# A feed-forward in two phases: seven block products per pair of weight tiles, and a pass through DRAM between up and down projection

## The chip, the core and the metric

The kernel runs on one core of one Trainium2 chip. The metric is the device time of one execution in microseconds (us), as a median over runs. TensorE (PE) multiplies a stationary 128x128 weight tile with up to 512 moving columns and adds into one of eight PSUM banks. VectorE (DVE), ScalarE (ACT) and GpSimd (POOL) work elementwise on 128 partitions, and SyncE (SP) and ACT issue the DMAs here.

## The reference, cut to what matters

A trunk of two layers works on 1024 latent tokens and 256 context tokens with 1024 features. Each layer has four parallel mixers, an output projection, a second norm and a feed-forward with 2816 hidden features. In the last layer only latent tokens go through the output projection and the feed-forward.

```python
def conv_ffn(h, w_up, conv_w, w_down):
    u, g = jnp.split(h @ w_up, 2, axis=-1)
    return (jax.nn.silu(dwconv(g, conv_w)) * u) @ w_down
...
        x = x + ml[2][:, None] * y_lat
        h2 = modulate(rmsnorm(x, norm2[l]), ml[3][:, None], ml[4][:, None])
        x = x + ml[5][:, None] * conv_ffn(h2, ffn_w_up[l], ffn_conv_w[l], ffn_w_down[l])
```

`dwconv` is a convolution of width 3 along the tokens, for each feature by itself.

## The kernel before, in words

All activations are feature-major: 128 features on the partitions, tokens along the free axis, eight such tiles (KT = 8) for 1024 features. The tokens come in groups (0, 256) context, (256, 512) and (768, 512) latent; the last layer drops the first. The kernel is written in a framework that orders the instructions of each engine ahead of the run, by priority (the order of the program text) and by its own timing model, and gives tiles of one tag a fixed number of buffers. A tile that finds no free buffer waits for the last reader of an old one.

**Products in three passes.** Each float32 operand is split into a float32r part and the rest (`split`: ACT casts `hi`, then POOL or DVE subtracts `lo`). `dense_acc` (L238) adds, for each of the eight feature tiles, hi·hi (L242), hi·lo (L243) and lo·hi (L244). So 24 matmuls make one 128-feature output tile of one token group. `load_w` (L226) loads a weight tile of 128x1024 (512 KB), and splits it: cast at L202, `lo` at L203 on `K.lo_eng`.

**Feed-forward.** `ffn` (L1650) walks over the 22 hidden tiles of 128 in blocks of two. For hidden tile j: the product `g` into `ps_g`, copied by ACT to `gp` (L1671); the convolution `conv3` (one ACT tap at L659, two DVE taps at L662 and L663); a SiLU (L1677); the product `u` into `ps_u`; DVE multiplies it with the convolved gate (L1683) and the result is split into `fh` and `fl`, three buffers each. After two hidden tiles, `down` multiplies both with their rows of `w_down` for all eight output tiles and all groups, and `resid` (L1601) adds each PSUM result, scaled, into the residual `x` in SBUF. The hidden features never leave SBUF. With the last block `done` runs the next norm (or the final norm and the store).

**Around it.** Before the feed-forward of a layer, the output projection (`dense_late`) is done for the first groups, then for the last group, and `norm_mod` normalises a group when its residual is complete. In layer 0, the parameters of the next layer's state-space mixer (`s5.scal`, `mats`, `turns`, `outs`: small DVE operations above all) are computed beside the first nine blocks of the feed-forward: `scal` in one go, the others in steps.

## Time and profile before

| | |
|---|---|
| time, median of 3 runs | 3555.32 us (3553.36 to 3558.95) |
| span of the profiled execution | 3550.2 us |
| feed-forward of layer 0 | about 988 to 1908 us of the span |
| feed-forward of layer 1 | about 2797 to 3527 us of the span |
| PE busy | 3418.2 us (96%) |
| DVE, ACT, POOL busy | 1708.2, 1106.9, 889.9 us |

The profile gives no time of its own for the profiled execution beside its span. The median of the runs is 5.1 us above that span; where a span is turned into a time, these 5.1 us are added. A busy share is an average over stages, so the stages are read one by one.

### The profile page before, as it was taken

Reading aid. Unit: us, or ns where it says so; the run is one execution under the profiler, and the core shown is the slowest. Engines: PE = TensorE matmul, PEld = TensorE weight load, DVE = VectorE, ACT = ScalarE, POOL = GpSimd, SP = SyncE. Lnnn points to the kernel's source line nnn. Section 1 sums busy time; section 2 is a strip of 40 time slices with the busy share of each in tenths; the row PEclk is TensorE's granted clock in tenths of the full one; section 3 lists DMA queues with packets and bytes.
Section 4 is the critical chain, followed back from the end, with each engine's and each line's share of the span. In section 5 each row is a group of like instructions: output and inputs, shape, how many; then the busy total and the mean of one; then the engine's idle time right before and its main releaser. Section 6 shows DMA issues by size and latency. Waiting matters only on the chain. (4 is left out here: it accounts for less than half of the span.)

```text
span 3550.2 us, 48986 instructions
## 1 busy us (share of the span) xinstructions
PE 3418.2 (96%) x19154; PEld 2795.2 (79%) x19186; DVE 1708.2 (48%) x3597; ACT 1106.9 (31%) x1885; POOL 889.9 (25%) x1061
## 2 busy tenths in 40 slices
PE   8899998999999999999999999998999999999998
PEld 6888995676768888888887889985666688888885
DVE  6857727554365486333323563636633432232333
ACT  4224534334242211111223324533333312212222
POOL 1922424011033222222221011331110223323321
PEclk9899998999999999999999999998999999999999
DMA  5577533345111121111112655542153111111111
GB/s 200 166 205 229 156 119 113 110 140 212 65 46 62 54 90 72 36 36 36 42 40 81 162 166 164 142 150 67 60 204 107 42 42 54 53 42 54 48 46 62
DMA packets 264904, 352.84 MB, mean 99 GB/s; under 512 B 89240, under 2 KB 190304, under 8 KB 264672
## 3 DMA queue, kind: packets, MB, share of 16 engines
q1 hardware_dynamic: 168148, 265.90, 23.5%
q10 hardware_dynamic: 96524, 83.81, 7.5%
q8 instruction: 151, 2.47, 0.3%
q14 instruction: 81, 0.66, 0.1%
HBM read 266.09 MB, written 83.52 MB: 98 GB/s over the span
## 5 line engine op out<-in xcount | busy, mean ns | idle before, releaser
L1601 DVE SCALAR_TENSOR_TENSOR x<-pd,modv,x 128x512 f32<-128x512 f32 (+1 forms) x448 | 299.8, 687 | 233.6 <-PE pd L244 233.2
L242 PE MATMUL pd<-fh,wh_d 128*128 128x512 f32 (+1 forms) x896 | 325.3, 369 | 9.3 <-ACT fh L202 5.7
L242 PE MATMUL ps_g<-hb,wh_g 128*128 128x512 f32 (+1 forms) x880 | 326.0, 370 | 3.2 <-ACT hb L214 2.2
L244 PE MATMUL ps_g<-hb,wl_g 128*128 128x512 f32 (+1 forms) x880 | 324.4, 369 | 2.5 <-POOL wl_g L203 2.5
L243 PE MATMUL pd<-fl,wh_d 128*128 128x512 f32 (+1 forms) x896 | 326.0, 367 | 0.7 <-POOL fl L203 0.7
L244 PE MATMUL pd<-fh,wl_d 128*128 128x512 f32 (+1 forms) x896 | 325.5, 368 | 0.0
L242 PE MATMUL ps_u<-hb,wh_u 128*128 128x512 f32 (+1 forms) x880 | 325.4, 370 | 0.0
L243 PE MATMUL ps_g<-hb,wh_g 128*128 128x512 f32 (+1 forms) x880 | 325.1, 369 | 0.0
L243 PE MATMUL ps_u<-hb,wh_u 128*128 128x512 f32 (+1 forms) x880 | 324.7, 369 | 0.0
L244 PE MATMUL ps_u<-hb,wl_u 128*128 128x512 f32 (+1 forms) x880 | 324.3, 369 | 0.2 <-POOL wl_u L203 0.2
L662 DVE SCALAR_TENSOR_TENSOR cv<-gp,vec,cv 128x1281 f32<-128x1281 f32 (+1 forms) x44 | 72.6, 1651 | 476.8 <-ACT cv L659 476.8
L242 PE MATMUL ps_in<-ha,wh_in 128*128 128x384 f32 (+3 forms) x688 | 218.3, 326 | 13.5 <-ACT st L1426 13.5
L203 POOL TENSOR_TENSOR wl_u<-wr_u,wh_u 128x1024 fp32r<-128x1024 f32 x44 | 105.5, 2397 | 481.7 <-ACT wh_u L202 481.7
L243 PE MATMUL ps_in<-ha,wh_in 128*128 128x384 f32 (+3 forms) x688 | 222.4, 323 | 0.0
L244 PE MATMUL ps_in<-ha,wl_in 128*128 128x384 f32 (+3 forms) x688 | 221.2, 322 | 0.0
L242 PE MATMUL ps_in<-hb,wh_in 128*128 128x256 f32 (+1 forms) x704 | 212.7, 305 | 0.8 <-ACT hb L214 0.6
L244 PE MATMUL ps_in<-hb,wl_in 128*128 128x256 f32 (+1 forms) x704 | 212.8, 303 | 0.0
L243 PE MATMUL ps_in<-hb,wh_in 128*128 128x256 f32 (+1 forms) x704 | 212.5, 302 | 0.2 <-DVE hb L215 0.2
L242 PEld LDWEIGHTS pd<-fh,wh_d 128*128 128x128 f32 x896 | 169.1, 189 | 45.8 <-DVE x L1601 7.4
L202 ACT CAST wh_u<-wr_u 128x1024 fp32r<-128x1024 f32 x44 | 46.3, 1051 | 502.4 <-PE pd L243 436.5
L242 PEld LDWEIGHTS ps_g<-hb,wh_g 128*128 128x128 f32 x880 | 166.2, 189 | 36.4 <-ACT hb L214 3.5
L243 PEld LDWEIGHTS pd<-fl,wh_d 128*128 128x128 f32 x896 | 169.4, 189 | 31.9 <-issue 1.7
(509 smaller groups left out, 7691.2 us busy)
## 6 DMA issues: line engine op xcount, KB each, us to landing
wm<-in_w_mod SPq DMA_DIRECT2D x96, 512.0 KB
wr_in<-in_w_in SPq DMA_DIRECT2D x44, 512.0 KB
wr_g<-in_w_up SPq DMA_DIRECT2D x44, 512.0 KB
wr_u<-in_w_up SPq DMA_DIRECT2D x44, 512.0 KB
wr_d<-in_w_down SPq DMA_DIRECT2D x44, 512.0 KB
wr_out<-in_w_out SPq DMA_DIRECT2D x32, 512.0 KB
PF<-st ACTq DMA_DIRECT2D x100, 128.0 KB
PF<-st ACTq DMA_DIRECT2D x60, 192.0 KB
```

The source lines that it names most:

```text
L202: nc.scalar.copy(hi, src)
L203: (eng or nc.gpsimd).tensor_tensor(lo, src, hi.bitcast(F32), OP.subtract)
L242: nc.tensor.matmul(ps, whi(k), ahi(k), start=start and i == 0, stop=False)
L243: nc.tensor.matmul(ps, whi(k), alo(k), start=False, stop=False)
L244: nc.tensor.matmul(ps, wlo(k), ahi(k), start=False, stop=stop and i == len(ks) - 1)
L662: nc.vector.scalar_tensor_tensor(dst, src[:, 0:n], w0, dst, OP.mult, OP.add)
L1601: nc.vector.scalar_tensor_tensor(v, ps, K.modv[l][:, 8 * part + m, c:c + 1], v, OP.mult, OP.add)
```

## The change

The feed-forward becomes two functions. `ffn_up` makes all 22 hidden tiles of a layer and writes each (`u` times gate, float32) to the DRAM tensor `HD`. `ffn_down` reads them back, splits them, and multiplies them with `w_down` in blocks of 1, 3, 4, 4, 4, 4 and 2 hidden tiles. In between, the activations are given up and the residual, which went to the DRAM tensor `XS` after its norm, is loaded again.

In `ffn_up`, hidden tile 0 is made as before. For the other 21, the latent part of the pair (u, g) is a 2x2 block product: rows are the u and the g tile, the inner index is split into features 0-511 and 512-1023 (four tiles each), columns are the two latent groups. Eight block products of twelve matmuls become seven (a Strassen-Winograd scheme). Its weight sums are formed for each tile (four POOL operations on 128x512, then two more splits), its activation sums (`tops`) once in a layer by `norm_fast`, which takes the place of `norm_mod` for the last latent group and works on it in two halves of 256 tokens. Products share two accumulators: `x` receives four of them one after the other without a restart and is copied or added out in between, `z` receives two. The context tokens of layer 0 are multiplied as before, in full.

```diff
-    def dense_acc(self, ps, whi, wlo, ahi, alo, ks, start=True, stop=True):
+    def dense_acc(self, ps, whi, wlo, ahi, alo, ks, start=True, stop=True, check=True):
+    def norm_fast(self, l, xs, kept, act, tops, dsh, pool, t0, n):
...
+        for k in range(4):
+            sh = self.modv[l][:, 28 + k, 0:1]
+            b12, b22 = scaled(k), scaled(4 + k)
+            t1, t4 = kept[k][:, d], kept[4 + k][:, d]
+            t2 = temp(f"n2{k}")
+            nc.vector.tensor_tensor(t1, b12, t1, OP.subtract)
+            stt(t2, b22, sh, t1, OP.add, OP.subtract)
+            self.split(t2, *[v[k][:, d] for v in tops[2]], nc.gpsimd)
+            self.split(t1, hi[k][:, s], lo[k][:, s], nc.gpsimd)
+            stt(b12, b22, dsh[:, k:k + 1], b12, OP.add, OP.subtract)
+            self.split(b12, *[v[k][:, d] for v in tops[3]], nc.gpsimd)
+            h = hi[4 + k][:, s]
+            nc.scalar.activation(h, b22, AF.Identity, bias=sh)
+            stt(lo[4 + k][:, s], b22, sh, h.bitcast(F32), OP.add, OP.subtract)
+            stt(t4, t4, sh, t2, OP.add, OP.subtract)
+            self.split(t4, *[v[k][:, d] for v in tops[4]], nc.vector)
...
-        K.wb = (1, 3)
-        wp = cw.enter_context(pool_(tc, name=f"w3{l}", bufs=3))
+        K.wb = (2, 4)
+        wp = cw.enter_context(pool_(tc, name=f"w3{l}", bufs=4))
...
+            for m in range(4):
+                K.dense(A["w_out"][l, m], act, KT, LAT[1:], resid(x, 2, m), wp, f"out{l}_{m}_768")
+            ws = [K.load_w(A["w_out"][l, m], KT, wp, f"out{l}_{m}_768") for m in range(4, 8)]
+            for t0, n in ((768, 256), (1024, 256)):
+                for m, (hi, lo) in zip(range(4, 8), ws):
...
+                norm(t0, n)
+        K.lo_eng = nc.gpsimd
+        with pool_(tc, name=f"w4{l}", bufs=3) as wq, pool_(tc, name=f"u{l}", bufs=1) as pool:
+            ffn_up(K, l, act, tops, HD, (wp, wq), pool)
+        ct.close()
+        cact.close()
...
+            x = open_x(c3, groups, "xx", side="right")
+            for t0, n in groups:
+                nc.sync.dma_start(x[t0], XS[:, :, t0:t0 + n])
+            s5s = s5[1] if l == 0 else None
+            stages = [(None, 0), (s5s.scal, 0), (s5s.mats, 8), (lambda p: s5s.turns(p, eng=nc.vector), 8), (s5s.outs, 8)] if s5s else []
+            with pool_(tc, name=f"f{l}", bufs=1) as pool:
+                for i, (b0, b1) in enumerate(((0, 1), (1, 4), (4, 8), (8, 12), (12, 16), (16, 20))):
...
+            if not last:
+                cact, act = open_act(f"c{l}")
+            with pool_(tc, name=f"fz{l}", bufs=1) as pool, pool_(tc, name=f"ez{l}", bufs=1, side="right") as ep:
+                ffn_down(K, l, range(NFF - 2, NFF), groups, lambda m: resid(x, 5, m), HD, wp, pool, iter(()), done(x, act), ep)
-def ffn(K, l, act, groups, resid, done, s5, wp):
...
+def ffn_up(K, l, act, tops, HD, wps, pool):
...
+        ur, gr = load("u", j), load("g", NFF + j)
+        uw = split("u", ur)
+        if j:
+            s12 = raw("s")
+            gt(s12[:, 4:], gr[:, :4], gr[:, 4:], OP.add)
+            gt(s12[:, :4], s12[:, 4:], ur[:, :4], OP.subtract)
+            w12 = split("s12", s12, 0, nc.vector)
+            gt(ur[:, :4], ur[:, :4], gr[:, :4], OP.subtract)
+            gt(ur[:, 4:], ur[:, 4:], s12[:, :4], OP.subtract)
+            w34 = split("s34", ur, 0, nc.vector)
+        gw = split("g", gr, 0 if full or not j else 4)
...
+            x = bank(K.pd, "px")
+            prod(x, uw, 0, B11, True)
+            put(ua, x)
+            y = bank(K.pb, "py")
+            prod(y, uw, 4, B21, True)
+            add(ua, y)
+            if full:
+                context(bank(K.pa, "pcu")[:, :TC], uw, u[:, :TC])
+            prod(x, w12, 0, tops[2], False)
+            put(ub, x)
+            z = bank(K.pb, "pz")
+            prod(z, w12, 4, T1, True)
+            put(gb, z)
+            prod(x, w34, 0, tops[3], False)
+            add(gb, x)
+            prod(z, w34, 4, B22, False)
+            add(ub, z)
+            prod(x, gw, 4, tops[4], False)
+            put(ga, x)
+            if full:
+                context(bank(K.pa, "pcg")[:, :TC], gw, gp[:, 1:1 + TC])
...
+        nc.scalar.dma_start(HD[j][:, h0:], u[:, h0:])
+def ffn_down(K, l, js, groups, resid, HD, wp, pool, steps, done=None, spool=None):
...
+    for j in js:
+        raw = pool.tile([P, T], F32, tag="hr", name=f"hr{l}_{j}", bufs=2)
+        nc.sync.dma_start(raw[:, h0:], HD[j][:, h0:])
+        wd.append(K.load_w(A["w_down"][l, j], KT, pool if j % 3 == 0 and not done else wp, f"d{l}_{j}"))
+        h = pool.tile([P, T], F32R, tag="fh", name=f"fh{l}_{j}", bufs=2 if done else 6)
+        lo = pool.tile([P, T], F32R, tag="fl", name=f"fl{l}_{j}", bufs=2 if done else 6)
+        for t0, n in groups:
+            s = slice(t0, t0 + n)
+            K.split(raw[:, s], h[:, s], lo[:, s], nc.vector)
...
+        for m in range(KT):
+            for t0, n in groups:
+                down(m, t0, n)
+            next(steps, None)
```

In `ffn_up`, `prod` is twelve matmuls (four feature tiles, three passes), `put` an ACT copy out of PSUM, `add` a DVE addition out of PSUM into the same place. The rest of the diff takes comments out, cuts the buffers of the loaded mixer outputs (`yraw`) from four to two, and makes the scratch space for DMA descriptors smaller.

## Rows read from the trace of the kernel before

**Rows 1.** The page, busy time and share of each engine.

```profile
PE 3418.2 (96%) x19154; PEld 2795.2 (79%) x19186; DVE 1708.2 (48%) x3597; ACT 1106.9 (31%) x1885; POOL 889.9 (25%) x1061
```

**Rows 2.** Windows: span; busy PE, PEld, DVE, ACT, POOL; clock; DMA.

```profile
988.00:1908.00 920.00, 908.09 (x4741) 774.07 (x4740) 432.58 (x958) 212.73 (x281) 245.95 (x221) 0.99 0.15 51
...
2680.00:2797.00 117.00, 112.94 (x457) 79.79 (x455) 45.99 (x50) 39.92 (x55) 13.49 (x11) 0.98 0.27 95
2797.00:3527.00 730.00, 726.03 (x3198) 592.46 (x3196) 244.07 (x288) 177.32 (x217) 213.59 (x171) 0.99 0.13 45
```

**Rows 3.** Timeline of PE in layer 0: start, duration (us), line, operation.

```profile
1042.27 0.28 PE L243 MATMUL ps_u<-hb,wh_u 128*128 128x256 f32 x1
...
1044.42 0.28 PE L243 MATMUL ps_u<-hb,wh_u 128*128 128x256 f32 x1
...
1045.12 0.39 PE L243 MATMUL ps_u<-hb,wh_u 128*128 128x512 f32 x1
...
1054.88 0.39 PE L244 MATMUL ps_u<-hb,wl_u 128*128 128x512 f32 x1
```

**Rows 4.** Waits of PE, 990 to 1100 and 1300 to 1400: total, times, longest.

```profile
PE pd L242 <- ACT fh L202: 5.7, 1, 5.7
...
PE pd L242 <- DVE x L1601: 3.6, 1, 3.6
```

**Rows 5.** Waits of PE 2660 to 2830, then one window (columns of rows 2).

```profile
PE ps_g L242 <- ACT hb L214: 2.2, 1, 2.2
...
2800.00:2810.00 10.00, 10.00 (x34) 7.79 (x34) 9.12 (x14) 4.27 (x7) 0.00 (x0) 0.72 0.00 0
```

**Rows 6.** Groups by form: count, busy us, mean ns, idle before.

```profile
L1601 DVE SCALAR_TENSOR_TENSOR x<-pd,modv,x 128x512 f32<-128x512 f32 x344 | 253.6, 749 | 211.5 <-PE pd L244 211.3
...
L203 DVE TENSOR_TENSOR wl_in<-wr_in,wh_in 128x1024 fp32r<-128x1024 f32 x44 | 56.2, 1277 | 51.2 <-ACT wh_in L202 50.5 <-PE ps_in L244 0.5
...
L1601 DVE SCALAR_TENSOR_TENSOR x<-pd,modv,x 128x256 f32<-128x256 f32 x104 | 49.9, 481 | 22.0 <-PE pd L244 21.9
...
L1671 ACT COPY gp<-ps_g 128x512 f32<-128x512 f32 x88 | 51.4, 584 | 214.2 <-PE ps_g L244 192.5 <-DVE z_cur L1044 14.1 <-DVE zt_TT L1236 7.3
...
L202 ACT CAST wh_u<-wr_u 128x1024 fp32r<-128x1024 f32 x44 | 46.3, 1051 | 502.4 <-PE pd L243 436.5 <-PE ps_u L243 53.0 <-PE ps_out L243 4.8
...
L203 POOL TENSOR_TENSOR wl_u<-wr_u,wh_u 128x1024 fp32r<-128x1024 f32 x44 | 105.5, 2397 | 481.7 <-ACT wh_u L202 481.7
```

**Rows 7.** Timelines of DVE and POOL in layer 1.

```profile
3134.74 1.29 DVE L662 SCALAR_TENSOR_TENSOR cv<-gp,vec,cv 128x1024 f32<-128x1024 f32 x1 [12.05 <-ACT cv L659]
3135.82 2.46 POOL L203 TENSOR_TENSOR wl_g<-wr_g,wh_g 128x1024 fp32r<-128x1024 f32 x1 [4.39 <-ACT wh_g L202]
3136.06 3.30 DVE L663 SCALAR_TENSOR_TENSOR cv<-gp,vec,cv 128x1024 f32<-128x1024 f32 x1
...
3103.27 1.30 POOL L203 TENSOR_TENSOR fl<-cv,fh 128x512 fp32r<-128x512 f32 x1
3103.63 2.07 DVE L1601 SCALAR_TENSOR_TENSOR x<-pd,modv,x 128x512 f32<-128x512 f32 x3 [2.99 <-PE pd L244]
```

**Rows 8.** Timeline of DVE in layer 0: parameters of the state-space mixer.

```profile
1030.56 0.18 DVE L1003 TENSOR_TENSOR z_mag<-z_are,z_dt 128x32 f32<-128x32 f32 x1
...
1059.21 0.19 DVE L1045 TENSOR_TENSOR z_cur<-z_cur,z_sqa 128x32 f32<-128x32 f32 x1
...
1277.72 0.18 DVE L1183 COPY zt_TT<-zt_sm 128x64 f32<-128x64 f32 x1
...
1281.86 0.19 DVE L1183 COPY zt_TT<-zt_sm 128x64 f32<-128x64 f32 x1
```

**Rows 9.** A 512 KB load, issue and first reader; a window (columns as rows 2).

```profile
869.79 0.33 SPq L230 DMA_DIRECT2D wr_out<-in_w_out  x1
...
872.99 1.05 ACT L202 CAST wh_out<-wr_out 128x1024 fp32r<-128x1024 f32 x1 [0.24 <-DMA wr_out<-in_w_out]
...
810.00:820.00 10.00, 10.00 (x86) 6.74 (x84) 6.96 (x13) 6.37 (x13) 0.73 (x1) 1.00 1.03 402
```

More of the change, by code (lines that the diff above doesn't have):

```diff
@@ L1 @@
+import functools
+import itertools
 from contextlib import ExitStack
@@ L69, in __init__ @@
         self.lo_eng = tc.nc.gpsimd
+        self.ntmps = 2
     def dump(self, name, ap, t0=0):
@@ L203, in split, with norm_apply @@
         (eng or nc.gpsimd).tensor_tensor(lo, src, hi.bitcast(F32), OP.subtract)
-    def norm_apply(self, l, which, k, x, rb, act, t0, n, pool):
+    def norm_apply(self, l, which, k, x, rb, act, t0, n, pool, keep=False):
         nc = self.nc
@@ L210, in norm_apply @@
         sh = self.modv[l][:, 24 * which + k, c:c + 1]
-        tmp = pool.tile([P, 512], F32, tag="ntmp", name=f"nt{l}{which}_{t0}_{k}", bufs=2)
+        if keep:
+            tmp = pool.tile([P, 512], F32, name=f"nk{l}{which}_{k}")
+        else:
+            tmp = pool.tile([P, 512], F32, tag="ntmp", name=f"nt{l}{which}_{t0}_{k}", bufs=self.ntmps)
         nc.vector.scalar_tensor_tensor(tmp[:, :n], x, self.ns[l][:, which, k, c:c + 1], rb, OP.mult, OP.mult)
@@ L1361 @@
 ALL_GROUPS = [(0, 256), (256, 512), (768, 512)]
+LAT = ALL_GROUPS[1:]
 def trunk(ctx, tc, A, out, dbg=None):
@@ new lines, in ffn_down, with down @@
+def ffn_down(K, l, js, groups, resid, HD, wp, pool, steps, done=None, spool=None):
+    nc, A = K.nc, K.A
+    h0 = groups[0][0]
+    nb = len(js)
+    fh, fl, wd = [], [], []
+    for j in js:
[7 more added lines that the diff above has]
+            K.split(raw[:, s], h[:, s], lo[:, s], nc.vector)
+        fh.append(h)
+        fl.append(lo)
+    def down(m, t0, n):
+        ps = K.acc(f"pd{l}_{js[0]}_{m}_{t0}")
+        K.dense_acc(ps[:, :n], lambda k: wd[k][0][:, m], lambda k: wd[k][1][:, m], lambda k: fh[k][:, t0:t0 + n], lambda k: fl[k][:, t0:t0 + n], nb)
+        resid(m)(ps[:, :n], t0, n)
+    if not done:
+        for m in range(KT):
+            for t0, n in groups:
+                down(m, t0, n)
+            next(steps, None)
+    else:
+        for t0, n in groups[:-1] + ([groups[-1]] if l == 0 else [(768, 256), (1024, 256)]):
+            for m in range(KT):
+                down(m, t0, n)
+            done(t0, n, spool)
```

254 lines of the change are left out of this document (148 added, 106 removed).

## The prediction, made before the changed kernel ran

> **What bounds the kernel now.** I read the page's busy table first: PE is busy 96% of the span, the next engine half of that [rows 1]. An average over stages can mislead, so the windows come next. In the feed-forward of layer 0 PE is busy 908 of 920 us, in layer 1 726 of 730 [rows 2]. A busy PE need not be at its peak, so the timeline has to show how close the matmuls stand: 43 starts of 128x512 in 9.76 us are 0.227 us each, 18 of 128x256 in 2.15 us are 0.119 us each [rows 3]. By these steps the matmuls of the code give 22 x (144 x 0.227 + 72 x 0.119) = 908 us for layer 0 and 22 x 144 x 0.227 = 719 us for layer 1. The windows hold 920 and 730: the feed-forward is a gapless stream of matmuls, and the reader should take from it that a removed matmul is worth its whole 0.227 us, as long as nothing else becomes late. The waits of PE show what little is late today: 5.7 us for `fh` and 3.6 us for `x` in layer 0 [rows 4], both while DVE computes the parameters of the next layer's mixer, and 2.2 us for `hb` at the start of layer 1, behind which the granted clock stands at 0.72 over ten microseconds, a mixture of its two levels of 1.2 and 2.4 GHz [rows 5].
>
> **What is removed.** One block product of eight is twelve matmuls of 512 columns, 12 x 0.227 = 2.72 us [rows 3]. 21 tiles in two layers: 42 x 2.72 = 114.4 us less. The context products, the down products and hidden tile 0 keep their columns. The two waits of rows 4 vanish at their old place: 9.3 us less. What causes them is moved and is priced below.
>
> **What is added on PE.** Four output tiles of each layer are made in halves of 256: 4 x 24 x (2 x 0.119 - 0.227) x 2 layers = 2 us more.
>
> **The other engines in the up phase**, for one hidden tile of layer 1, in which PE needs 84 x 0.227 = 19.1 us. POOL: one `lo` of 1024 at 2.40 us, four sums of 512 at half of that, half a `lo`: 8.4 us. ACT: three and a half casts at 1.05, four copies at 0.58, one tap and a SiLU of 1024 taken like casts: 8.1 us. DVE: two `lo` at 1.28, three additions at about 0.75, two taps at 1.29 [rows 6, 7] and a multiplication of 1024 at about 1.28: 8.7 us. None is near 19.1, and layer 0 adds 5.7 us of PE for less work on the others, so the sums of weights cost nothing as long as they run a tile ahead. Six buffers for four split pairs allow that. If this cover goes, one pair late costs a cast and a POOL `lo`, 3.5 us.
>
> What can be late is the shared accumulator. Product 3 may not touch `x` before ACT copied it, product 7 not before DVE added it out, and each has one product of 2.72 us as slack. DVE works in order, and what stands ahead of the addition can be held up: a tap that takes 1.29 us took 3.30 us while POOL's 2.46 us `lo` ran, whereas three evacuations that read PSUM beside a POOL operation took their normal 2.07 us [rows 7]. Behind the late addition stands product 7, and all of PE with it. Bounds: nothing if the slack holds, and for each tile 2.40 + 1.28 - 2.72 = 0.96 us ahead of one addition plus 3.30 + 1.29 - 2.72 = 1.87 us ahead of another, 2.8 us x 42 = 119 us. POOL runs for 8.4 of 19.1 us, and an operation must be both held up and just ahead of an addition, so I take a value close to the lower end, 10 us.
>
> A rule of the Trainium skill speaks against the change here. The page "SBUF — State Buffer", section "Who interferes with whom", says that a DVE instruction with two SBUF inputs and a GpSimd instruction that reads SBUF exclude each other for the whole instruction of the one that came first. Rows 7 agree. If every such pair met, by this rule DVE and POOL would work in turn, 8.7 + 8.4 = 17.1 of 19.1 us, which still fits; by the row alone the sum is the same.
>
> **Out projection to up phase.** Before, the last norm cost 2.2 us of waiting, smaller waits and a slow clock. Now the norm works in halves, but forms three sums: about eight DVE operations of 256 (0.48 us each [rows 6]) for each of four tile pairs, 15 us for each half, where PE has 8 x 12 x 0.227 / 2 = 10.9 us of hidden tile 0 that needs no result of it. I take 3 us more, between 7 us less and 15 us more (one whole half). The weights of tile 1 go where `x` and the norm's buffers lie and wait for them; that is within the upper end.
>
> **Up phase to down phase, once in each layer.** Loads of `x` and `HD` go where the activations and `tops` lie, so they wait for the last products. A load of 512 KB took 872.99 - 869.79 = 3.2 us to its reader [rows 9]; cast and `lo` of the first groups and of the weights (1.05 + 2.40 us) follow. The `x` loads, 5.2 MB, stand ahead on SP's queue: 13 us at the 402 GB/s of rows 9, while evacuation, not the first product, waits for them. Bounds for a layer: 0 if the loads slip in before the last products, 20 us (13 + 3.2 + 3.5) if all stands in a row. PE's clock may halve behind a gap, as in rows 5. Between the ends I take 8 us in layer 0, where the context product reads all activations to the end, and 6 us in layer 1.
>
> **Down phase.** PE needs 24 x (0.119 + 2 x 0.227) = 13.8 us a hidden tile in layer 0, and fewer, longer accumulations take evacuations off DVE. But the parameters of the mixer, beside nine blocks before, now lie beside hidden tiles 1 to 15. DVE in the first five blocks: 5 x (16 x 0.749 + 8 x 0.481) = 79 us of evacuations, 16 x 1.6 = 26 us of `lo` [rows 6], `scal` 29 us (1030.6 to 1059.2), `turns` 8 x 4.14 = 33 us, and `mats` and `outs` taken like `turns`, their nearest row [rows 8]: 233 us against 16 x 13.8 = 220 us of PE. So DVE is the bound there, by 13 us. Bounds: 0, since durations overlap and a little may slide into the block after, and 13 + 16 x 2.4 = 51 us if each POOL `lo` of 2.40 us also holds DVE. I take 15 us. Layer 1 has no such work.
>
> At the edge of a block, the third and fourth tile's buffers are free only when the old block ends: a cast and a POOL `lo`, 3.5 us, against 0 if PE goes on with other banks (five are in use). Ten edges: 0 to 35 us, I take 10. The last block lies in a new pool; in layer 0 its loads overlay buffers of the block before: 3.2 us for a load and some 3 us for cast and `lo`, 6 us, and 2 in layer 1; bounds 0 and 16. The stores of `HD` and `XS` go by ACT's queue and are read much later: nothing.
>
> **The sum.** -114.4 - 9.3 + 2 + 10 + 3 + 14 + 15 + 10 + 8 = -61.7 us. From the span of 3550.2 that gives 3488.5, and with the 5.1 us around it about **3494 us**, against a median of 3555.3.
>
> **Rivals.** (1) *All is hidden*: every added term at its lower end, -114.4 - 9.3 + 2 - 7 = -129 us, 3427 us. For it speaks that the order of each engine is planned and PE waits almost nowhere today. Against it: the loads between the phases cannot start before the buffers are free. 7%. (2) *Slower, by the shared accumulator*: 2.8 us a tile where I took 0.24 adds 109 us: 3603 us. It decides above 0.24 + 61.7 / 42 = 1.7 us of PE wait a tile. The 3.30 us of rows 7 speaks for it, the low load of DVE and POOL against it. The rule quoted above is this rival's mechanism. 8%. (3) *No change, by the phase borders*: loads, block edges and last block at their upper ends, 40 + 35 + 16 instead of 32: 3553 us. For it speaks that these waits have no cover in the program, against it that a block of 55 us leaves ample time to load the next. 7%. That the change does not remove the products is not in doubt from the code.
>
> **Chances and range.** My forecast has 78%; its own spread comes from the 0 to 51 us of DVE in layer 0 and the 0 to 40 us between the phases, 3440 to 3545 us. As a range this leaves out rivals 1 and 2 and some two thirds of rival 3 (the rest of it falls a little short of its upper ends), 7 + 8 + 5 = 20 of a hundred. A measurement of this kernel tells 0.2%, 7 us, from no change. Faster: 78 + 7 + 3 (rival 3 where it falls short) = 88%. Same: the other 4% of rival 3. Slower: 8%.
>
> **What the profile after would show.** PE busy some 112 us lower and the matmuls still 0.227 us apart; in the up phase 84 matmuls of 512 columns a tile and no repeating wait of PE on an ACT copy or a DVE addition; two gaps of 5 to 10 us on PE where `HD` is first read; DVE above 9 tenths in the first quarter of layer 0's down phase, with PE waiting for `x` or `fl`; gaps of a microsecond at block edges. The prediction is wrong if PE waits for `x` or `z` in every tile, if the first down product comes more than 20 us after the last up product, or if the matmuls of the up phase stand further apart.

## The result: 1.5% slower, and the profile after

After the change the median is 3606.8 us against 3554.9 us for the kernel before on the same chip: a ratio of 1.0147, 95% interval 1.0132 to 1.0161, 52 us slower where 61 us faster was forecast. The span of the profiled execution is 3601.3 us, 51 us above that of before; its time is 3603.1 us, so 1.8 us lie outside the span; if before was alike, the other 3.3 of the prediction's 5.1 us are spread between executions.

The busy table of the page, after (answers to [rows 1]):

```profile
PE 3349.4 (93%) x18906; PEld 2726.7 (76%) x18906; DVE 1946.9 (54%) x3825; ACT 1256.6 (35%) x2167; POOL 1068.1 (30%) x1043
```

PE is busy 69 us less and the span is 51 us longer: 120 us of idle time are new. (69 and not 112: the up phase's matmuls stand wider apart, some 10 us in all, and the mean granted clock is 0.965 in place of 0.981, so that some matmuls take longer. The two shares were not measured apart.) The windows of the kernel after say where; columns as in [rows 2]. For the first, the kernel before stood at

```profile
880.00:900.00 20.00, 20.00 (x111) 17.34 (x110) 10.59 (x12) 5.77 (x6) 0.00 (x0) 1.00 0.68 250
```

and after:

```profile
880.00:900.00 20.00, 9.07 (x30) 6.25 (x30) 4.17 (x6) 5.18 (x8) 3.16 (x3) 0.66 0.72 256
...
1050.00:1080.00 30.00, 3.86 (x23) 3.08 (x22) 29.12 (x54) 14.60 (x37) 17.01 (x23) 0.58 0.10 35
...
1100.00:1600.00 500.00, 499.97 (x2625) 428.14 (x2624) 189.96 (x179) 190.12 (x242) 225.48 (x120) 1.00 0.20 69
...
1620.00:1635.00 15.00, 0.00 (x0) 0.00 (x0) 6.58 (x10) 4.91 (x8) 2.27 (x3) 0.55 0.92 337
1635.00:1650.00 15.00, 6.22 (x16) 4.41 (x17) 10.66 (x21) 6.70 (x12) 14.18 (x4) 0.50 0.61 216
...
1672.00:1692.00 20.00, 20.00 (x107) 17.22 (x106) 19.23 (x96) 0.00 (x0) 0.31 (x1) 1.00 0.26 91
...
2850.00:2880.00 30.00, 2.57 (x7) 1.78 (x8) 28.44 (x52) 14.79 (x35) 16.57 (x23) 0.50 0.10 35
2900.00:3290.00 390.00, 390.00 (x1693) 317.42 (x1692) 206.53 (x161) 158.12 (x200) 216.48 (x117) 1.00 0.23 80
3300.00:3312.00 12.00, 0.00 (x0) 0.00 (x0) 5.61 (x5) 3.74 (x6) 2.05 (x1) 0.53 1.04 409
```

In the up phase, the two long windows, PE does not idle: the new work itself runs nearly as forecast. The time is lost around it: in the output projection (880), at the norm (1050, 2850), where PE stands still while DVE is busy without a break, and between the phases (1620, 3300), where PE stands still and the DMA engines are full. The waits of PE name the same places (whole run; total, times, longest; answers to [rows 4] and [rows 5]):

```profile
PE pxu L285 <- ACT u L1803: 47.9, 2, 26.0
PE pd L285 <- ACT wh_d L205: 30.9, 2, 16.8
PE ps_out L285 <- ACT hb L205: 21.5, 10, 6.6
...
PE pd L285 <- DVE xx L1644: 13.2, 10, 4.0
PE pd L286 <- DVE fl L206: 6.9, 6, 1.8
```

No line for an accumulator `px` or `pz` is among them. To locate the loss I set the same marks in both traces (us from the span's start), `px` being the first block product:

| mark | before | after |
|---|---|---|
| first attention product of layer 0 | 593.5 | 597.7 |
| first, last product of layer 0's out projection | 835.7, 987.0 | 862.1, 1030.0 |
| first `px`, last product of the up phase | none, 1907.5 | 1091.6, 1619.0 |
| first, last down product, layer 0 | 1055.1, 1945.1 | 1635.8, 1997.8 |
| last product of layer 1's out projection | 2775.8 | 2831.4 |
| first `px`, last product of the up phase | none, 3493.3 | 2893.4, 3298.7 |
| first, last down product, layer 1 | 2837.5, 3527.2 | 3312.8, 3578.0 |

From them follows the balance of the 51 us, beside the prediction's terms:

| stretch | measured | forecast |
|---|---|---|
| mixers and out projection, both layers (4.2 before the attention, 38.8 in layer 0 behind it, 5.2 in layer 1) | +48 | +2 |
| last out product to first `px`: 61.6 and 62.0 us for 28 and 22 us of products, 74 lost; before, from the last out product to the first down product, 130 us for 99 of products, 31 lost | +43 | +3 |
| up phase: -114.4 for the products, and 12 longer than 520.4 + 400.4 us | -102 | -104 |
| up to down: 16.8 and 14.1 us | +31 | +14 |
| down phase: 362.0 and 265.2 us for 303.6 and 239.7 us of products, 84 lost; 51 lost in the feed-forward before apart from the norm | +33 | +24 |
| layer 0 to layer 1 | -2 | 0 |

### The profile page after: what moved, and what is told of

It is laid out like the page before. It is cut to its first block, busy times and chain, and to the rows that moved or that the text cites. A ratio compares the mean times of both kernels' runs of the same rounds, so it can differ in the third digit from the quotient of the medians.

```text
span 3601.3 us, 49563 instructions
## 1 busy us (share of the span) xinstructions
PE 3349.4 (93%) x18906; PEld 2726.7 (76%) x18906; DVE 1946.9 (54%) x3825; ACT 1256.6 (35%) x2167; POOL 1068.1 (30%) x1043
## 5 line engine op out<-in xcount | busy, mean ns | idle before, releaser
L1644 DVE SCALAR_TENSOR_TENSOR xx<-pd,modv,xx 128x512 f32<-128x512 f32 (+1 forms) x288 | 191.8, 678 | 173.2 <-PE pd L287 172.2
L206 POOL TENSOR_TENSOR wl_d<-wr_d,wh_d 128x1024 fp32r<-128x1024 f32 x44 | 110.7, 2528 | 471.4 <-ACT wh_d L205 458.7
L285 PE MATMUL ps_in<-hc,wh_in 128*128 128x256 f32 (+1 forms) x704 | 211.5, 303 | 4.6 <-ACT hc L220 3.3
L286 PE MATMUL ps_in<-hc,wh_in 128*128 128x256 f32 (+1 forms) x704 | 212.6, 303 | 0.0
L287 PE MATMUL ps_in<-hc,wl_in 128*128 128x256 f32 (+1 forms) x704 | 212.6, 303 | 0.0
L287 PEld LDWEIGHTS pd<-fh,wl_d 128*128 128x128 f32 x896 | 172.1, 193 | 36.1 <-POOL wl_d L206 4.7
L206 POOL TENSOR_TENSOR wlo_u<-wr_u,whi_u 128x1024 fp32r<-128x1024 f32 x44 | 106.8, 2428 | 231.4 <-ACT whi_u L205 203.8
L947 DVE TENSOR_REDUCE a_mx<-a_pm 128x1 f32<-128x512 f32 (+1 forms) x200 | 114.0, 590 | 112.4 <-PE a_pm L946 110.5
L982 PE MATMUL a_po<-a_E,a_vt 128*128 128x512 f32 (+1 forms) x336 | 171.3, 596 | 2.8 <-ACT a_E L981 2.7
L285 PE MATMUL ps_out<-hb,wh_out 128*128 128x256 f32 (+1 forms) x384 | 131.1, 358 | 25.8 <-ACT hb L205 21.5
L285 PEld LDWEIGHTS ps_in<-ha,wh_in 128*128 128x128 f32 x688 | 131.9, 192 | 17.4 <-ACT st L1470 13.9
```

What stands on the lines that cost most here:

```text
L206: (eng or nc.gpsimd).tensor_tensor(lo, src, hi.bitcast(F32), OP.subtract)
L285: mm(ps, whi(k), ahi(k), start=start and i == 0, stop=False)
L286: mm(ps, whi(k), alo(k), start=False, stop=False)
L287: mm(ps, wlo(k), ahi(k), start=False, stop=stop and i == len(ks) - 1)
L947: nc.vector.tensor_reduce(mx[:, c, j:j + 1], ps[:, :kw], mybir.AxisListType.X, OP.max)
L982: nc.tensor.matmul(po[:, :w], vt[:, kt, hp, 64 * ho:64 * ho + P], E[:, :w], start=kt == 0, stop=kt == kts[-1])
```

## The experiments

All but `ey_actlo` do the whole computation. Ratios are to the kernel before on the same chip, with 95% intervals; 1 us is 0.00028. Marks and stretches are read from one trace of each kernel.

**Is the block scheme worth anything?** `plain8` keeps both phases, makes eight plain products and normalises the last group as before, without the sums.

```diff
-        if j:
+        if 0:
...
-            x = bank(K.pd, "px")
-            prod(x, uw, 0, B11, True)
...
+                K.dense_acc(ps, lambda k: w[0][:, k], lambda k: w[1][:, k], lambda k: act[0][k][:, t0:t0 + n], lambda k: act[1][k][:, t0:t0 + n], KT)
+                put(dst, ps)
```

> Two phases as in the changed kernel, but all hidden tiles made by eight plain block products and the last latent group normalised by the old norm (in two halves). Theory 'borders': the seven products do save their 114 us in the up phase, and what eats them is the work at the borders, of which the activation sums in the norm are one: the up phase grows by 114 us, the two gaps before hidden tile 0's second half (26 and 30 us of idle PE, some 15 us of slow clock behind them) shrink to some 10 us in all, so 3607 + 114 - 60 = about 3660 us. Rival 'scheme': the shared accumulators and sums of weights cost as much as they save; then plain products are no slower than the changed kernel, 3607 us or less.

Measured: 1.0327 [1.031, 1.0344]. Against 1.0147 the scheme gives back 0.018 or 64 us of its 114; the two phases without it cost 116 us, with all that comes along (place in memory, a new instruction order). From the last out product to the last up product its trace has 618 and 491 us for 605 and 479 us of products: without the sums some 25 us are lost in that stretch and not 86 (74 at the norm, 12 in the up phase). So the loss is not in the sums and shared accumulators of the 42 tiles, but in what the phases need around them and in the 43 us at the norm.

**Why does the out projection start late?** Its input loads (`yraw`) on SP's queue and their first cast, after:

```profile
815.54 0.89 SPq L1674 DMA_DIRECT2D yraw<-YD  x2
...
859.94 10.55 SPq L1674 DMA_DIRECT2D yraw<-YD  x6
```

```profile
858.69 0.93 ACT L205 CAST hb<-yraw 128x256 fp32r<-128x256 f32 x2
```

Before:

```profile
794.37 2.55 SPq L1610 DMA_DIRECT2D yraw<-YD  x4
```

Two things differ: two buffers in place of four, and where the split activations lie: the weight pool below them grew by 12 KB a partition, which by the program text moves them onto memory that the attention still holds. `early_y` shrinks the pool again, shares out the other weight buffers to fit, makes five whole output tiles in place of four for the last group, and gives `yraw` four buffers; `before_y2` takes the buffers alone away from the kernel before.

```diff
-        K.wb = (2, 4)
-        wp = cw.enter_context(pool_(tc, name=f"w3{l}", bufs=4))
+        K.wb = (1, 3)
+        wp = cw.enter_context(pool_(tc, name=f"w3{l}", bufs=3))
...
-                            raw = wo.tile([P, 512], F32, tag="yraw", name=f"yraw{l}_{k}_{t0}", bufs=2)
+                            raw = wo.tile([P, 512], F32, tag="yraw", name=f"yraw{l}_{k}_{t0}", bufs=4)
```

> The changed kernel with the memory of its weight buffers in the order of before (wp with 1 raw and 3 split buffers, the missing ones in the up phase's and down phase's own pools) and four buffers for the loaded mixer outputs in place of two. Theory: the out projection starts late because these loads and their splits find no free memory before the attention ends; with it they run beside the attention again, the first out product starts some 25 us earlier in layer 0 and some 10 earlier in layer 1, and the time falls by 25 to 40 us to about 3575 us. Rival: the attention itself ends later in the changed kernel and the out projection has to wait for it; then the time stays within 5 us of 3607.

> The kernel before with two buffers instead of four for the loaded mixer outputs, nothing else. Theory 'place in memory': what made the loads late in the changed kernel is that the activations lie 12 KB higher, on memory that attention still holds; two buffers alone cost little, within 6 us of the kernel before. Rival 'two buffers': each load waits for a split two loads back, the out projection of layer 0 starts some 25 us later and the time rises by 20 us or more.

`before_y2` 1.0012 [1.0003, 1.0021]: in the kernel before, the buffers cost next to nothing. `early_y`: the casts begin at 821.4 in place of 858.7, and the window that was half empty is full:

```profile
880.00:900.00 20.00, 19.68 (x112) 16.95 (x111) 11.99 (x15) 6.16 (x8) 1.32 (x1) 1.00 0.66 233
```

The out projection of layer 0 ends at 997.1 in place of 1030.0, with the attention begun at the same time (597.6). So 33 us of this stage hung on what `early_y` changes, and since the buffers alone cost little, the place in memory is the likelier cause; it was not changed by itself. But the time is 1.0141 [1.0126, 1.0156], as before within the error. At the first `px` of layer 0 the trace has 22 of the 33 us left (the wait at the norm grew to 30.6 us), at layer 1's last out product 20, at the end 8. The next tries ask what holds the norm.

**What holds the sums at the norm?** Four tries: the squares' buffers (`ey_sq4`, four in place of two; the same edit on the change itself, `sq4`, gave no result, since its buffers do not fit), the order of the out projection (`ey_halves`, all eight output tiles by halves of 256, so that the first half's norm runs under the second; `ey_whole`, one piece of 512), or the pace of the DVE chain (`ey_actlo`, the three POOL subtractions of `norm_fast` become ACT copies). All stand on `early_y`.

```diff
-            sq = sqs(f"sq_{name}_{i}") if sqs else pool.tile([P, 512], F32, tag="sq", name=f"sq_{name}_{i}", bufs=bufs)
+            sq = sqs(f"sq_{name}_{i}") if sqs else pool.tile([P, 512], F32, tag="sq", name=f"sq_{name}_{i}", bufs=self.nsq or bufs)
```

> early_y with four buffers instead of two for the squares of the second norm. early_y brought the last out product forward by 33 and 20 us, but hidden tile 0's second half by only 23 and 21, and the longest wait of PE grew to 30.6 us. Theory 'queue on DVE': the norm of the first latent group (16 us of DVE) stands ahead of the two halves of the sums only because its sums of squares are read late; with four buffers it runs while DVE is idle, the wait shrinks by 10 to 16 us a layer: 3600 - 25 = about 3575 us. Rival: PE's fixed order between out products sets when squares are read: 3600 within 5 us.

1.0139 [1.0122, 1.0156], no gain. The norm of the first latent group was done 12 us earlier in layer 0, and the sums of the last group began when they did before, 15 us behind the last out product.

```diff
+                for m in range(KT):
+                    K.dense(A["w_out"][l, m], act, KT, [(t0, n)], resid(x, 2, m), wp, f"out{l}_{m}_{t0}")
```

> early_y, but all eight output tiles of the last latent group are made in two halves, first half for all eight, norm, then second half (four more weight loads and splits a layer, 2 us more of PE in all). Theory 'too little cover': DVE needs 18 us for the sums of one half, and PE has 8.6 us of out products beside the first half; with 23 us beside it the first half is hidden and only the second stands against hidden tile 0: the wait falls from 31 and 27 us to some 15 and 15: 3600 - 25 = about 3575 us. Rival 'DVE bound': what counts is the whole DVE work behind the residuals, its start does not move: 3600 within 5 us.

1.0299 [1.0272, 1.0326], 56 us worse than `early_y`. The waits of PE, whole run:

```profile
PE pxu L285 <- ACT u L1798: 36.6, 2, 19.2
PE ps_out L285 <- ACT wh_out L205: 25.1, 20, 2.2
...
PE ps_out L287 <- DVE wl_out L206: 14.3, 17, 4.0
```

The wait at the norm shrank as meant (61.0 to 36.6 us in two layers), but every weight tile now serves 256 columns only, and PE waits for casts and rests of the weights in the out projection (39 us on these two lines).

```diff
-            for m in range(5):
+            for m in range(KT):
...
+                norm(*LAT[1])
```

> early_y, but the output projection and the norm of the last latent group in one piece of 512 tokens instead of two of 256. In early_y the sums run at 4.45 us for each of eight tile pairs of 256, and start 14 us after the last out product, the first half's too: the halves overlap with nothing. Theory 'DVE chain': four tile pairs of 512 at some 7 us end 6 to 8 us earlier in each layer, and PE saves the halves' 2 us: 3600 - 15 = about 3585 us. Rival: in one piece the first sums start later by the 8.6 us that the halves gave them, no gain: 3600 within 5 us.

1.0147 [1.0133, 1.0161], no gain: operations of twice the length, 8.2 us a pair of tiles against 2 x 4.45, and they begin later.

```diff
-            self.split(t2, *[v[k][:, d] for v in tops[2]], nc.gpsimd)
-            self.split(t1, hi[k][:, s], lo[k][:, s], nc.gpsimd)
+            self.split(t2, *[v[k][:, d] for v in tops[2]], "act")
+            self.split(t1, hi[k][:, s], lo[k][:, s], "act")
```

> early_y, where the three rests that POOL subtracts for each tile pair of the sums (of T1, T2 and T3) are not subtracted but filled by copies of ACT: that part of the computation is left out, all else is as it was. Theory 'DVE and POOL exclude each other': of the 4.45 us a pair some 1.4 are three DVE operations of 0.94 us in place of 0.47 beside a running POOL subtraction; without POOL a pair takes 3.1 to 3.7 us, and the wait of PE before hidden tile 0's second half shrinks by 6 to 10 us in each layer: 3600 - 16 = about 3584 us. Rival: the DVE operations take 0.94 us for another reason, the pace stays at 4.45 us and the time at 3600 within 5.

1.0068 [1.0051, 1.0084], 26 us better than `early_y`. A pair of tiles in the kernel after, on DVE and POOL (timeline):

```profile
1070.01 0.41 DVE L252 TENSOR_TENSOR nk<-nt,nk 128x256 f32<-128x256 f32 x1
1070.68 0.47 DVE L253 SCALAR_TENSOR_TENSOR n<-nt,modv,nk 128x256 f32<-128x256 f32 x1
1071.00 0.74 POOL L206 TENSOR_TENSOR hb<-nk,hb 128x256 fp32r<-128x256 f32 x1 [1.59 <-ACT hb L205]
1071.07 0.95 DVE L256 SCALAR_TENSOR_TENSOR nt<-nt,dsh,nt 128x256 f32<-128x256 f32 x1
1071.70 0.90 POOL L206 TENSOR_TENSOR top02l<-n,top02h 128x256 fp32r<-128x256 f32 x1
1071.94 0.94 DVE L260 SCALAR_TENSOR_TENSOR hb<-nt,modv,hb 128x256 fp32r<-128x256 f32 x1
1072.57 0.90 POOL L206 TENSOR_TENSOR top03l<-nt,top03h 128x256 fp32r<-128x256 f32 x1
1072.81 0.94 DVE L261 SCALAR_TENSOR_TENSOR nk<-nk,modv,n 128x256 f32<-128x256 f32 x1
...
1074.46 0.41 DVE L252 TENSOR_TENSOR nk<-nt,nk 128x256 f32<-128x256 f32 x1
```

and in `ey_actlo`:

```profile
1034.00 0.42 DVE L255 TENSOR_TENSOR nk<-nt,nk 128x256 f32<-128x256 f32 x1
...
1035.07 0.48 DVE L259 SCALAR_TENSOR_TENSOR nt<-nt,dsh,nt 128x256 f32<-128x256 f32 x1
1035.47 0.48 DVE L263 SCALAR_TENSOR_TENSOR hb<-nt,modv,hb 128x256 fp32r<-128x256 f32 x1
1035.86 0.48 DVE L264 SCALAR_TENSOR_TENSOR nk<-nk,modv,n 128x256 f32<-128x256 f32 x1
...
1037.05 0.42 DVE L255 TENSOR_TENSOR nk<-nt,nk 128x256 f32<-128x256 f32 x1
```

The same three DVE operations take 0.94 us beside POOL's subtractions and 0.48 without them (in the kernel after, the five with no POOL operation beside them took 0.47); pairs follow each other after 4.45 and 3.04 us, eight of them 36 and 24 us. This DVE chain, with POOL in its way, is the largest part of the wait at the norm.

**And the buffers of the first tile?** After the chain, in the kernel after:

```profile
1078.32 0.17 POOL L1755 MEMSET gp<- 128x1 f32 x3 [0.40 <-DVE nk L261]
1078.54 0.58 ACT L1803 COPY u<-pxu 128x512 f32<-128x512 f32 x1
```

The products ahead of that copy had ended by 1051; it waits for `u`, which lies on the norm's memory. `ey_preu` gives the first `u` and `gp` memory of their own, opened before the norm.

```diff
+            cu = ExitStack()
+            pu = cu.enter_context(pool_(tc, name=f"u0{l}", bufs=1))
+            pre = pu.tile([P, TPAD], F32, name=f"gp{l}_0"), pu
...
-        u = pool.tile([P, T], F32, tag="u", name=f"u{nm}", bufs=2)
+        u = (pool if j % 2 else pre[1]).tile([P, T], F32, tag="u", name=f"u{nm}", bufs=1)
```

> early_y, but the buffers of the first hidden tile's results (u and gp) have memory of their own instead of lying where the norm's buffers lie. In the changed kernel the clearing of gp and the copy of u out of PSUM run within a microsecond of the norm's last write, though the products they wait on ended 36 us earlier. Theory 'memory': the copy runs at once, PE goes on with the second half of hidden tile 0 as the norm delivers it, and some 8 of its 11 us hide in the norm: 3600 - 16 = about 3584 us. Rival 'order': ACT's fixed order puts the copy behind the norm's casts anyway: 3600 within 5 us.

1.0082 [1.006, 1.0104], 21 us better than `early_y`. The copy now stands at

```profile
1010.82 0.59 ACT L1807 COPY u<-pxu 128x512 f32<-128x512 f32 x1
```

in place of 1047.4 in `early_y`. From the last out product to the first `px` it gains 5 us in layer 0 (72.6 to 67.2) and 9 in layer 1 (60.9 to 51.9), less than the 36 us of the copy: what follows it waits for the norm's results in any case, as the waits of PE show (layer 0, 1000 to 1075 us).

```profile
PE pxu L285 <- ACT hb L205: 20.2, 4, 13.0
```

The other gains lie elsewhere: layer 0's down phase 367.2 to 353.3 us, the gap of layer 1 between the phases 17.4 to 9.4.

**Between the phases.** Loads, first cast and first down product of layer 0, after:

```profile
1605.03 7.27 SPq L1727 DMA_DIRECT2D xx<-XS  x2
1618.87 0.52 SPq L1727 DMA_DIRECT2D xx<-XS  x1
1622.57 0.48 SPq L1869 DMA_DIRECT2D hr<-HD  x1
```

```profile
1632.01 1.45 ACT L205 CAST fh<-hr 128x256 fp32r<-128x256 f32 x3 [5.60 <-DMA hr<-HD]
1634.67 1.04 ACT L205 CAST wh_d<-wr_d 128x1024 fp32r<-128x1024 f32 x1 [1.22 <-DMA wr_d<-in_w_down]
...
1635.77 0.58 PE L285 MATMUL pd<-fh,wh_d 128*128 128x256 f32 x1 [16.81 <-ACT wh_d L205]
```

The last 2 MB of `x` go out with the last up product and `HD` stands behind them. `hd_first` puts the `x` loads behind block 0's own loads in the program text; `ey_hd2` does this on `early_y`, and sends block 0's `HD` through ACT's queue. Both make block 0's products group by group.

```diff
-            for t0, n in groups:
-                nc.sync.dma_start(x[t0], XS[:, :, t0:t0 + n])
+            def xload():
+                for t0, n in groups:
+                    nc.sync.dma_start(x[t0], XS[:, :, t0:t0 + n])
...
-        nc.sync.dma_start(raw[:, h0:], HD[j][:, h0:])
+        (nc.scalar if first else nc.sync).dma_start(raw[:, h0:], HD[j][:, h0:])
```

> The changed kernel with the loads of the down phase's first hidden tile and its weights put ahead of the loads of the residual, its weights in the pool that is free earlier, and its products group by group. Theory: the first down product waits behind 2 MB of residual on the DMA engines (9.4 us from issue to use, where a load alone takes 3.2); it comes 8 us earlier in each layer: about 3591 us. Rival: the 5.2 MB of the residual are a floor of 13 us, since the results need it anyway and five banks fill at once; then 3607 within 5 us.

> early_y with the down phase's first rows of HD loaded by ACT's queue instead of SP's, its weights in the pool that is free earlier, and its products group by group. In hd_first the rows still stood behind a weight load on SP that waited 3.7 us for its buffer and behind 2 MB of residual. Theory: by its own queue the load lands at 4 to 5 us behind the last up product, and the two gaps fall from 16.6 and 17.4 to about 8 us: 3600 - 18 = about 3582 us. Rival 'volume': 5.2 MB of residual at 400 GB/s are 13 us whatever the order: within 5 us of 3600.

`hd_first` 1.0136 [1.0117, 1.0156], gaps 13.6 and 11.9 in place of 16.8 and 14.1 us. `ey_hd2` 1.0112 [1.0096, 1.0128]; its gap in layer 0 stayed at 16.1 us. But neither shows what another order is worth: the framework planned the loads of `x` ahead all the same. In `hd_first`, where the last up product ends at 1622.6:

```profile
1622.49 0.52 SPq L1728 DMA_DIRECT2D xx<-XS  x1
...
1626.18 0.76 SPq L1870 DMA_DIRECT2D hr<-HD  x1
```

In `ey_hd2`, ACT's queue issued `HD` 9.4 us behind the last up product of layer 0, after the store of the last hidden tile. The DMA engines are full at this border (0.92 and 1.04 in the windows above), but the volume of the residual is not what sets the gap: `plain8` loads it more than 480 us earlier, and its gaps are 12.2 and 11.9 us with the DMA engines little more than half busy. Its border in layer 0:

```profile
1652.90:1665.10 12.20, 0.06 (x2) 0.03 (x1) 7.07 (x10) 6.34 (x8) 2.46 (x3) 0.64 0.53 196
```

As far as this pair shows, the volume explains 4.6 and 2.2 us; in `plain8` too `HD` is issued only 3.9 us behind the last up product, and lands and is split after that. No run issued it before. What `ey_hd2` gained lies in the down phase of layer 0, 352.5 against 367.2 us.

**All of them, and one layer only.** `ey_all` adds up `ey_sq4`, `ey_halves` and `ey_hd2`. `l1_only` leaves layer 0 as it was, `l1_best` too, on `early_y` and `ey_hd2`:

```diff
+        if l == 0:
...
+                ffn(K, l, act, groups, resid, done, s5[1] if l == 0 else None, wp)
+            continue
```

> The edits of early_y, ey_sq4, ey_halves and ey_hd2 together. Theory: the gains add where they are in different places, but the two for the norm share one wait: 3600 - 35 - 18 = about 3547 us, the time of the kernel before. Rival: each gain is given back at the next border: 3580 us or more.

> Layer 0 as in the kernel before, layer 1 as in the changed kernel. In the traces layer 1 takes 1581 us from its first input product to the end in both kernels, while layer 0 is 50 us longer in the changed one. Theory 'layer 0 loses, layer 1 breaks even': the time of the kernel before, 3550 us within 8. Rival 'the layers lose alike' (the trace of one execution misleads by noise in the mixers): some 25 us above the kernel before.

> Layer 0 as in the kernel before, layer 1 with the edits of best1. l1_only was 20 us above the kernel before. Theory: the edits take 13 us off the norm and the phase border of layer 1; what stays is about 12 us by which layer 0's mixers run longer in all kernels with changed code behind them: 3554 + 7 = about 3561 us. Rival: layer 1 gains nothing, since its out projection was hardly late: 3574 us.

`ey_all` 1.0272 [1.0252, 1.0292]: it carries the loss of `ey_halves`. `l1_only` 1.0059 [1.0046, 1.0071] and `l1_best` 1.0047 [1.0034, 1.006] are slower than the kernel before, but hardly slower than `null` below (1.0041), in which no layer is changed. From the last out product of layer 1 to its last down product their traces have 743 and 741 us, `null` 750 and the kernel before 751: here the change gains 8 to 10 us. What is lost lies ahead, in the mixers and the out projection.

**The best of the parts.** `best1` is `early_y`, `ey_preu` and `ey_hd2`; `best1_plain` is the same with eight products. `best1_warm` puts twelve spare matmuls on PE behind the last up product; `best2` forms the three rests on DVE and starts the mixer's parameters a block later (both on `best1`).

```diff
+        pw = K.pa.tile([P, 512], F32, tag="m", name=f"warm{l}")
+        for _ in range(12):
+            nc.tensor.matmul(pw[:, :384], K.ident, K.cst.rearrange("p a b -> p (a b)"), start=True, stop=True)
```

```diff
-            self.split(t2, *[v[k][:, d] for v in tops[2]], nc.gpsimd)
+            self.split(t2, *[v[k][:, d] for v in tops[2]], nc.vector)
...
-            stages = [(None, 0), (s5s.scal, 0), (s5s.mats, 8), (lambda p: s5s.turns(p, eng=nc.vector), 8), (s5s.outs, 8)] if s5s else []
+            stages = [(None, 0), (None, 0), (s5s.scal, 0), (s5s.mats, 8), (lambda p: s5s.turns(p, eng=nc.vector), 8), (s5s.outs, 8)] if s5s else []
```

> early_y with the edits of ey_preu and ey_hd2 together. Theory 'the gains add' (21 us of ey_preu, 9 of ey_hd2, in different places but for the gap between the phases): about 3574 us, 20 us above the kernel before. Rival: both shorten the same down phase of layer 0 (14 us in each), so that ey_preu's 21 us is all: about 3580 us.

> best1 with eight plain block products and the old norm of the last latent group. plain8 was 63 us slower than the changed kernel, 51 short of the 114 that 42 block products are worth. Theory: half of these 51 went where best1 mended them (copy of the first results, 8 to 10 us of the norm in each layer), so the scheme is worth more here: best1 + 75 = about 3645 us. Rival: the mended borders help the plain products as much: best1 + 63 = 3633 us or less.

> best1 with twelve products of 384 float32 columns on constants, whose result nobody reads, between the last up product and the first down product of each layer. Theory 'slow clock': PE's clock stays high through the gap, and the first down products, which ran at half speed for some 15 us in the changed kernel, run at full speed: 8 to 12 us less than best1 in all. Rival: the first down products wait for loads and evacuations anyway; no change within 4 us, or some us more where the filler runs past the gap.

> best1 with the three rests of each tile pair of the sums subtracted by DVE instead of POOL, and the mixer's parameters begun one block of the down phase later. Theory: the pace of the sums was 3.04 us a pair where POOL did none of them (ey_actlo); three more DVE subtractions at 0.41 us make 4.27 instead of 4.45, 1 to 2 us a layer, and the first three blocks of layer 0's down phase, in which DVE is busy 19 of 20 us, lose 3 to 8 us of waits: 3570 - 8 = about 3562 us. Rival: the parameters only collide with later blocks, and the sums are as long: 3570 within 4.

`best1` 1.0043 [1.0029, 1.0057]: the gains add up, 37 us better than the change as it was. `best1_plain` 1.0251 [1.0237, 1.0266]: the scheme is worth 74 us there. `best1_warm` 1.0079 [1.0063, 1.0094] is worse; its windows in layer 0:

```profile
1595.00:1605.00 10.00, 9.25 (x31) 5.44 (x30) 4.90 (x4) 4.55 (x5) 4.36 (x2) 1.00 0.91 321
1605.00:1612.00 7.00, 0.00 (x0) 0.00 (x0) 0.50 (x1) 0.83 (x1) 0.00 (x0) 0.75 1.02 387
1612.00:1625.00 13.00, 8.27 (x30) 7.01 (x31) 12.20 (x15) 7.50 (x13) 10.58 (x6) 0.63 0.70 243
```

The filler ran out 8.3 us before the first down product, and the granted clock fell all the same; without it `best1` has 0.71 in the 13 us from its first down product on. In layer 1 the framework planned the filler into the wait at the norm (2817 to 2826 us) and not to the border: from the last out product to the first `px` it takes 62 us there, in `best1` 51. That is most of the loss, so a filler at the border of layer 1 was not tested. `best2` 1.0059 [1.0045, 1.0072], no gain: what POOL no longer does, DVE now does in the same chain, at 4.1 us a pair. In layer 0, from the last out product to the last down product, it is 7 us shorter than `best1` (947 against 954), and 14 us longer between there and the last out product of layer 1.

**What does rebuilding the instruction order cost by itself?** `null` has the old `ffn` and out projection in both layers, inside the changed program text (which also has the smaller scratch space for DMA descriptors); PE does the work of before.

```diff
+        if True:
+            cw = ExitStack()
+            K.wb = (1, 3)
...
+                ffn(K, l, act, groups, resid, done, s5[1] if l == 0 else None, wp)
+            continue
```

> The changed file with output projection, norm and feed-forward of the kernel before in both layers: the same work, in an order that the framework plans anew. Theory 'order': the mixers run some 5 us longer in each layer, 3554 + 10 = about 3564 us, and layer 0's first attention product comes 4 to 10 us later than in the kernel before. Rival: the delay belongs to the new feed-forward behind the mixers; then 3554 within 3 us.

1.0041 [1.0027, 1.0055]: 15 us without any change of work. The order of PE's instructions agrees with that of before for the first 490 only (DVE 122, ACT 31), and the mixers of layer 0 are already late at the first attention product. First `null`, then the kernel before with two `yraw` buffers:

```profile
605.68 1.05 PE L982 MATMUL a_po<-a_E,a_vt 128*128 128x256 f32 x2
```

```profile
593.30 1.22 PE L939 MATMUL a_po<-a_E,a_vt 128*128 128x256 f32 x2 [0.26 <-ACT a_E L938]
```

That is 12 us; the out projection of layer 0 then ends at 1004.0, 17 us later than before, and the feed-forward stretches are those of before (921 us from the last out product to the last up product, as before).

The edit of the feed-forward is not what re-orders the mixers, for `null` has none. The eighteen traces of kernels made from the changed file have one order of ACT and DVE instructions up to 740 us at least, whatever their edits, while `before_y2` keeps the order of before up to 807 us, where its edit lies. So the new order comes from something that all these files share and the kernel before lacks; the smaller scratch space is one candidate, and no run changes it alone. With this one order the first attention product comes at 597.6 to 610.0 us in the eighteen traces, so the 12 us of `null` are also a matter of the execution.

So `best1` and `null` are equal: mended, the change is worth nothing in all, and as it was it costs 0.0106 or 38 us against the same early order. They are not equal piece by piece: from the last out product to the last down product `best1` is 4 and 7 us shorter than the kernel before (954 and 744 against 958 and 751 us), and between the last down product of layer 0 and the last out product of layer 1 it is 10 us longer (841 against 831; `null` 832). No version here is faster than the kernel before.

## Why the prediction was wrong, point by point

**Right: what PE saves.** The up phase has no idle time and no wait for a shared accumulator, which I had priced at 10 us. Some of its matmuls stand a little further apart than [rows 3], which I had named as a sign against me: nine starts from 1300.92 to 1302.79 us, 0.234 us each. These read `tops`, as 36 of the 84 of a tile do.

```profile
1300.92 0.40 PE L285 MATMUL px<-top02h,whi_s 128*128 128x512 f32 x1
...
1302.79 0.40 PE L287 MATMUL px<-top02h,wlo_s 128*128 128x512 f32 x1
```

Together -102 us where -104 was forecast (-114.4, +10). That the sum is so close is luck: the 10 us were for waits that did not come, and 12 us came from elsewhere, some 10 of them from the wider steps (1512 x 0.0065). The weight sums took longer than I had taken, 1.45 to 1.84 us each in place of 1.2, and were covered:

```profile
L1786 POOL TENSOR_TENSOR wr_s<-wr_g 128x512 f32<-128x512 f32 x42 | 74.0, 1763 | 147.9 <-DVE wlo_s L206 145.2 <-issue 2.4
```

**Wrong: "Out projection to up phase", 3 us, bounds 7 less to 15 more.** It cost 43 us. The step took 15 us for a half's DVE operations at 0.48 us each and let 10.9 us of hidden tile 0 cover each half. Three things failed. Three of those operations take 0.94 us, since POOL's subtractions of the same sums run beside them; a pair takes 4.45 us instead of 3.8 by 0.48 each. The halves cover nothing for each other: the sums of both follow as one chain of 36 us, the first starting 10 to 12 us after the last out product. And hidden tile 0 covers less than I took, because its `u` and `gp` lie on the norm's memory (5 and 9 us, `ey_preu`). My upper end of "one whole half" was no upper end: both halves lie on the path. On the exclusion, the Trainium skill, page "SBUF — State Buffer", section "Who interferes with whom", says that a DVE operation with two SBUF inputs and a GpSimd operation that reads SBUF hold each other up; this trace agrees, 0.94 against 0.48 us. I had applied it to the up phase, where DVE and POOL have time to spare, and not to the norm, where they have none.

**Wrong: the out projection, priced at the 2 us of its halves.** It cost 46 us more. I had the cut of `yraw` to two buffers and the larger weight pool before me and priced neither. The buffers are harmless in the kernel before (`before_y2`); with the smaller pool the out projection of layer 0 ends 33 us earlier (`early_y`), likely because the 12 KB moved the activations onto the attention's memory. What is left, 10 to 15 us, is of the size of what `null` loses without any new work. That the changed file has another instruction order far ahead of the feed-forward was in none of my terms.

**Undersized: "Up phase to down phase", 14 us.** 31 us, within the bounds of 0 to 40. I took the middle because the loads might slip in before the last products. The first two `x` loads do, the third and `HD` do not: `HD` is issued 3.6 us behind the last up product in layer 0. The 13 us of the `x` loads at 402 GB/s, which made most of my upper end, are not the main part: `plain8` has gaps of 12 us without them. Neither gap reached the 20 us that I had named as proof against me.

**About right: the down phase**, 33 us for 24: DVE is at 9.6 tenths where forecast (window 1672), PE waits 13 us for `xx` and `fl` in layer 0 (forecast 15), and single waits for `fl` at three block edges are 1.3 to 1.9 us. The slow clock behind the gap, 0.50 in the window from 1635, I had named but not priced.

The misses, 46 + 40 + 17 + 9 + 2 - 2 = 112 us, are the distance between -61.7 and +50.8. Rival 2 named 3603 us, nearly the time that came, by a mechanism that did not occur: its place was the shared accumulator, the loss was at the borders. Rival 3 looked at the borders, but only at the loads between the phases, not at the norm and the out projection.

**Open.** Why matmuls that read `tops` stand 0.234 us apart; those with weight sums alone do not (0.227 to 0.230). What in the changed file re-orders the mixers. How much of a difference under some 10 us between two kernels here is the edit: the mixers before the first attention product, which no edit touches, moved by up to 12 us between traces with one order. `early_y` shows it most: 33 us gained in layer 0, 8 at the end. What sets the gap between the phases, of which the residual's volume explains the smaller part. That the wait at the norm can be removed without another loss was not shown; `ey_actlo` shortens it by leaving the rests out.

## What to carry to other kernels

A change that takes columns off a gapless TensorE pays only between its borders; price first what each border needs before the next product, as a chain with its own engine and pace, and give covers of two halves no credit before a row shows them overlapping. When a pool grows, look up what lies beneath the tiles that it pushes: a tile on memory that an earlier stage still holds can start late, whatever its own buffers. Where a planner orders the program, look in the trace whether an edit of order was taken over at all (two here were not), run the old work in the new text as a null, and trust no difference smaller than what that moves.

## What was not expected of the hardware

The same DVE operation on 128x256 took 0.47 to 0.48 us alone and 0.94 beside POOL operations of 0.90 us on the same partitions, and three POOL operations a pair stretched a DVE chain from 3.04 to 4.45 us. Spare matmuls ahead of a gap did not keep the clock: after 8.3 us without work the granted clock in the next 13 us was 0.63. The same work from the changed file, in another order of instructions and with a smaller scratch space for DMA descriptors, took 0.41% longer.
